# A two-level Winograd matrix product with GELU: one group's B operands are not stored but built again from B, and A is staged in other buffers

## The chip, the cores and the metric

The kernel runs on one core of a Trainium2 chip. The metric is the device time in microseconds (us) of one execution. Five engines work side by side, each through its own instruction stream in order: TensorE (PE, matrix products), VectorE (DVE), ScalarE (ACT), GpSimd (POOL) and SyncE (SP). Here POOL and SP mainly issue DMA transfers. An engine that waits for a semaphore holds up everything behind it in its own stream.

## The reference

```python
def reference(a, b):            # a, b: float32, 4096 x 4096
    x = np.matmul(a, b)
    return 0.5 * x * (1 + np.tanh(np.sqrt(2 / np.pi) * (x + 0.044715 * x**3)))
```

## The kernel before

**The arithmetic.** A, B and the output C are each cut into 2 x 2 quadrants of 2048 x 2048 ("11", "12", "21", "22"). One level of the Winograd form of Strassen's method makes the four quadrants of C from seven products instead of eight. A *group* is one block of C: 512 rows of the upper and 512 of the lower half, 512 columns of the left and 512 of the right half, over the whole depth. There are 4 row blocks (mb) and 4 column blocks (nb), so 16 groups, numbered 0 to 15. Groups 0-3 have mb 0 and nb 0, 1, 2, 3; groups 4-7 have mb 1 and nb 3, 0, 1, 2; groups 8-11 nb 2, 3, 0, 1; groups 12-15 nb 1, 2, 3, 0.

In a group the seven products are called P1 to P7. Each multiplies a 512 x 2048 left operand (a quadrant of A or a sum of some) with a 2048 x 512 right operand (a quadrant of B or a sum of some). P1, P2 and P3 take raw quadrants of B; P4 to P7 take sums. A *full* product has four quarters (q) along the depth, each of four row tiles: 64 matmuls of 128 x 128 by 128 x 512 (line 534). A *split* product applies the same method once more inside: seven quarter products of 16 matmuls with 256 columns (line 908), run in four stages, with four sums of the left operand, four of the right one ("pieces" 5, 6, 7, 4) and some adds and copies in the accumulators between the stages. Operands are float16; a sum of two operands is one DVE instruction over 128 x 2048 (line 838).

**Where B's operands come from.** Groups 1 to 5 are *raw groups* (`raw_group`, line 1293). They load the four quadrants of B for their nb, 64 DMAs of 128 KB on the POOL queue that cast float32 to float16 (`load_raw`, line 1166), and make the sums in place, on top of operands that are no longer needed. The first time that an nb comes up, the seven right operands are also written to DRAM as *units*, 4 x 512 KB each (`keep_`, `store_unit`, on the SP queue). An in-place sum must wait for the store of what it overwrites. Groups 3 and 4 share nb 3. Groups 6 to 15 are *late groups* (`late_group`, line 1407): they fetch units on the POOL queue. How a product is done there is a letter in the table `GROUPS`: no letter is full; "m" is split, with the pieces of the right operand summed in place; "ms" is split, with the pieces also stored to DRAM; "f" is split, with the pieces fetched from DRAM (seven transfers of 512 KB instead of four). `RAW_MAKES` lets group 5 make and store the pieces of P1, P2, P5 and P6 for nb 0.

**Buffers.** A quarter of an operand is a *cell* of 128 x 2048 float16 (512 KB). Cells 0 to 15 hold B (four slots; `bR` in the trace), 16 to 23 sums of A (`SB`, `SA`; `aD`), 24 to 27 the two stages (`ST`; `stage`). In late groups cells 0 to 15 are a pool: `new_cell` takes the first free one, and a fetch waits until the last reader of that cell is done. A transposed quadrant of A lies in four slots (`aT`). While the last group of a row block runs (groups 3, 7 and 11), A for the next row block comes in: `turn_quad` (line 1134) loads half a quadrant (four DMAs of 256 KB) into a stage, DVE transposes it into a slot of `aT` that is no longer used (line 411), and ACT squares it row by row for a check of magnitudes (line 1155). A quadrant's halves alternate between the two stages. In late groups that do not bring in A, the stages hold a sum of A, A11 - A21, the left operand of P7; groups 7 and 11 take four pool cells for that sum instead (`s3 = new_unit()`).

The first raw groups of an nb also sum the squares of B's elements for the same check: 32 ACT squares (line 1189) and 30 DVE adds (line 1194), placed by `SQUARES`.

**The order of the work.** PE's order is as the program writes it. The order on the other engines and on the two DMA queues is set while the kernel is built, by a planner (`Plan`, line 107): each operation has a duration from the table `COST` and each transfer a duration from `MOVE`, with a weight `HEAVY` for the share that a unit's transfer takes of the DMA engines while both queues move data. The planner runs through these durations, lets each engine take the most urgent operation that is ready, and writes down the order. So a different `MOVE` or `HEAVY` moves no work but can change the order on DVE, ACT, POOL and SP everywhere behind group 0.

The outputs leave through `out_of` and `out_from`: an ACT GELU (lines 1099 and 1109) and a 256 KB store on SP. A finished product's accumulators are copied out by ACT (line 1115) or added by DVE to what other products left (line 1121). Where P1 and P2 are full, ACT copies P1's result into P2's accumulators (line 1290), and P2 waits for that copy. In a raw group the products run in the order P1, P2, P5, P6, P7, P4, P3; in groups 7 and 11 P4 comes first.

Of the kernel before, what the change touches and what calls it, by code (L numbers as in the profile page):

```python
# [21 lines left out]
RUN = KC // 4  # L22
RT = 4
# [43 lines left out]
LAG = 0.2  # L67
MARGIN = 1.5
LANES = 8
MOVE = {"unit": 1.27, "out": 0.63, "raw_a": 1.25, "raw_b": 0.65, "tiny": 0.2}  # L70
HEAVY = 1.7
COST = {
    "full": 0.861, "half": 0.876, "wide": 0.983,
    "sum": 1.19, "sum/2": 0.66, "turn": 1.26, "add": 0.68, "add16": 0.69, "small": 0.35, "stat": 2.2,
# [7 lines left out]
def modes_of(tail=None, **kw):  # L82
# [1 line left out]
    return got if tail is None else {**got, "tail": tail}  # L84


RAW_MAKES = {5: ("P1", "P2", "P5", "P6")}
GROUPS = {
    6: modes_of(ms="P2 P5 P7"),
    7: {},  # L90
    8: modes_of(ms="P2 P5 P7"),
    9: modes_of(ms="P2 P5 P7"),
    10: modes_of(f="P1 P2 P5 P6", ms="P7"),
    11: modes_of(m="P5"),
    12: modes_of(f="P2 P5 P7", m="P1 P6"),
    13: modes_of(f="P2 P5 P7", m="P1 P6 P3"),
    14: modes_of(f="P2 P5 P7", m="P1 P6"),
    15: modes_of(f="P1 P2 P5 P6 P7", m="P3"),
}
TURNS = {7: 2, 11: 3}  # L100


# [188 lines left out]
def half_path(  # L291
# [461 lines left out]
    def dma(queue, dst, src, r, w, what, **kw):  # L753
        eng = {"POOL": nc.gpsimd, "SP": nc.sync}[queue]
        weight = HEAVY if what == "unit" else 1.0
        return plan.add(queue, COST[queue], lambda: eng.dma_start(out=dst, in_=src), r=r, w=w, size=MOVE[what],  # L756
                        weight=weight, **kw)

# [372 lines left out]
    rows = [pool.tile([P, 2, NX], F32, name="rows", tag=f"rows{ih}") for ih in range(2)]  # L1131
    seen_rows = set()

    def turn_quad(mb, quad, slot):
        ih, kh = int(quad[0]) - 1, int(quad[1]) - 1
        n = NX // 2
        t = rows[ih]
        for h in range(2):
            k = next_stage[0] % 2
            next_stage[0] += 1  # L1140
            s = stages[k].rearrange("p (x c) r -> p x (c r)", c=CH)
            toks = [c(24 + 2 * k), c(25 + 2 * k)]
            x0 = (ih * MH + mb * TM) // Q + h * n
            batch = (mb, quad, h)
            for g in range(4):
                dma("POOL", s[g * Q : (g + 1) * Q, :, :], a_v[kh, g, :, x0 : x0 + n, :], [], toks,
                    "raw_a", batch=batch)
            for cc in range(CH):
                src = s.rearrange("p x (c r) -> p c x r", c=CH)[:, cc]
                x = slice(h * n, (h + 1) * n)  # L1150
                dve("turn", lambda cc=cc, x=x, src=src: transpose(slot, cc, x, src), toks, [("a", slot, cc, h)])
            f = new_small()
            for x in range(n):
                r = h * n + x
                act("weigh", lambda x=x, r=r, s=s, f=f: nc.scalar.activation(  # L1155
                    small[f].bitcast(F16)[:, : 2 * RUN], s[:, x, :], ACT.Square, accum_out=t[:, kh, r : r + 1]),
                    toks, [("rows", ih), ("f", f)], batch=("w", mb, quad, h), slack=60.0)
            free_small.append(f)
        if (mb, ih) in seen_rows:
            dve("small", lambda: nc.vector.tensor_reduce(  # L1160
                out=stats["a"][:, (2 * mb + ih) * NX : (2 * mb + ih + 1) * NX],
                in_=t.rearrange("p k x -> p x k"), axis=AX.X, op=ALU.add,
            ), [("rows", ih)], [("sa", mb, ih)], slack=60.0)
        seen_rows.add((mb, ih))
# [69 lines left out]
        t = b_phys[x0 // 4, k].rearrange("p j n -> p j n")[:, :, w * HC : (w + 1) * HC]  # L1234
        return t, [c(x0 + 2 * k), c(x0 + 2 * k + 1)]

    spare, behind = [], {}

    def make_raw(nb, name, slot):

        x0 = slot * 4
        prev = {}

        def piece_sum(p, op, x, y):
            t = spare.pop(0)
            combine2(cell(t).rearrange("p (j n) -> p j n", n=HC), [c(t)], x, y, op)
            dma("SP", piece(nb, name, p)[:, :], cell(t), [c(t)], [("t", nb, name, p)], "unit")
            prev[p] = (cell(t).rearrange("p (j n) -> p j n", n=HC), [c(t)])
            spare.append(t)

        b11, b12, b21, b22 = (inner_of(x0, x) for x in ("11", "12", "21", "22"))
        piece_sum("7", -1, b22, b12)
        piece_sum("5", -1, b12, b11)
        piece_sum("6", -1, b22, prev["5"])
        piece_sum("4", -1, b21, prev["6"])
# [36 lines left out]

    def raw_group(gi, keep_units, makes, fetch=(), next_nb=None, turn=None):

        mb, nb = groups[gi]
        X, Y = 0, 1
        sl = dict(slots["b"])
# [15 lines left out]
        block(SB, 1, raw("21"), raw("22"))  # L1313
        block(SA, -1, raw("11"), raw("21"))
        if turn:
            turn_quad(turn, "11", slots["a"]["21"])
        sq("11")
        mk("P1", sl["11"])
        keep_("P1", s11)
# [30 lines left out]

        unsplit(Y, lambda q: a_quarter(blk(SB), q), lambda q: s11[q], True, None, t2)
        if turn:
            turn_quad(turn, "12", slots["a"]["11"])
        mk("P6", sl["11"])
        mk("P4", sl["21"])
        if (gi, "end") in SQUARES:
# [8 lines left out]

        unsplit(X, lambda q: a_quarter(blk(SB), q), lambda q: s11[q], False, u2, s4)
        if turn:
            turn_quad(turn, "21", slots["a"]["12"])
        if next_nb is not None:
            load_raw(next_nb, "11", sl["11"])  # L1370
        elif gi + 1 in REFETCH:
# [9 lines left out]
        unsplit(X, lambda q: a_quarter(blk(SA), q), lambda q: s12[q], False, u3)  # L1381
        if next_nb is not None:
            load_raw(next_nb, "21", sl["12"])
        unsplit(X, lambda q: a_quarter(raw("22"), q), lambda q: s21[q], False, lambda i: out_from(gi, i, 1, 0, X))
        if turn:
            turn_quad(turn, "22", slots["a"]["22"])
        if next_nb is not None:
            load_raw(next_nb, "12", sl["21"])
        elif gi + 1 in REFETCH:
            for q in range(QPH):  # L1390
                fetch_unit_to(nb, "P2", q, s21[q])
# [2 lines left out]
            add_bank(u[i], Y, i)  # L1394
            out_of(gi, i, 0, 1, u[i])

        unsplit(Y, lambda q: a_quarter(blk(SB), q), lambda q: s22[q], False, c12)
        if next_nb is not None:
            load_raw(next_nb, "22", sl["22"])
            slots["b"] = {"11": sl["11"], "21": sl["12"], "12": sl["21"], "22": sl["22"]}  # L1400
# [6 lines left out]
    def late_group(gi, modes, turn=None):  # L1407
# [7 lines left out]
        if new_mb:  # L1415
            block(SA, 1, raw("21"), raw("22"))
        block(SB, -1, blk(SA), raw("11"))
        if turn:
            s3 = new_unit()
            block(s3, -1, raw("11"), raw("21"))  # L1420
            turn_quad(turn, "11", slots["a"]["21"])
        else:
            s3 = ST
            if new_mb:
                block(ST, -1, raw("11"), raw("21"))
        source = {
            "P1": raw("11"), "P2": raw("12"), "P5": blk(SA), "P6": blk(SB), "P7": blk(s3), "P3": blk(SB), "P4": raw("22")
        }
# [50 lines left out]
        if turn:  # L1479
            def p4_done(i, s=X):  # L1480
                x4[i] = copy_out(s, i)

            run(work("P4", X, True, p4_done))
            turn_quad(turn, "22", slots["a"]["22"])
            X, Y = Y, X
        both(("P1", X, True, p1_done, "P6" not in cut), ("P2", Y, not alone, p2_done))
        if last:
            final_answer()
        if turn:
            turn_quad(turn, "12", slots["a"]["11"])  # L1490
        both(("P6", X, False, p6_done, not tail_v), ("P5", Y, True, p5_done, not tail_v))
        if last:
            final_read()
        block(SB, -1, raw("12"), blk(SB))
        if turn:
            turn_quad(turn, "21", slots["a"]["12"])

        def c12(i):
            f = v if tail_v else u
# [47 lines left out]
        if tail_v:  # L1547
            both(("P7", X, True, c22_v, True), ("P3", Y, True, c12))
            if turn:
                free_cells.extend(s3)  # L1550
                for i in range(RT):
                    c21_turn(i)
            else:
                run(work("P4", X, False, c21))
            sets["X"] = Y
        else:
            run(work("P7", X, False, c22))
            if turn:
                free_cells.extend(s3)
                for i in range(RT):  # L1560
                    c21_turn(i)
                run(work("P3", Y, False, c12))
            elif "P3" in cut:
                for i in range(RT):
                    add_bank(u[i], Y, i)
                run(work("P4", X, False, c21), work("P3", Y, True, c12))
            else:
                run(work("P4", X, False, c21))
                run(work("P3", Y, False, c12))
            sets["X"] = X  # L1570
        if turn:
            old = slots["a"]
            slots["a"] = {"11": old["21"], "12": old["11"], "21": old["12"], "22": old["22"]}

    N_RAW = 6
    REFETCH = (4,)
    SQUARES = {(1, q) for q in ("11", "12", "21", "22", "end")} | {(2, q) for q in ("11", "12", "21", "22", "end")}
    SQUARES |= {(3, "12")} | {(4, q) for q in ("11", "21", "22", "end")}
    SQUARES |= {(5, q) for q in ("11", "12", "21", "22", "end")}
    said = {}  # L1580

    def first_weights():
# [42 lines left out]
    with tc.manual_schedule():  # L1625
        nc.vector.memset(zeros[:, :], 0.0)
        first_group()
        behind[1, "P1"] = load_raw(1, "12", slots["b"]["12"])[:8]
        behind[1, "P2"] = load_raw(1, "22", slots["b"]["22"])[8:]
        first_weights()  # L1630
        raw_group(1, NAMES, (), next_nb=2)
        raw_group(2, NAMES, (), next_nb=3)
        raw_group(3, ("P1", "P2", "P5"), (), turn=1)
        spare.extend(ST)
        raw_group(4, ("P3", "P4", "P6", "P7"), (), fetch=("P5", "P7"), next_nb=0)
        raw_group(5, NAMES, RAW_MAKES[5])
        free_small.extend((4, 5, 6, 7))
        for slot in ("11", "12", "21", "22"):
            free_cells.extend(slot_cells(slots["b"][slot]))
        for gi, modes in GROUPS.items():  # L1640
            if gi == LAST:
                final_checks()
            late_group(gi, modes, TURNS.get(gi))
        plan.emit()
# [37 lines left out]
```

## Time and profile before

| | |
|---|---|
| Time, median of 3 runs | 1540.89 us (1539.96 to 1546.77) |
| The profiled execution's own time | 1545.48 us |
| Its span in the trace | 1543.6 us |
| Mean granted TensorE clock | 0.996 of full speed |
| PE idle in the span | 27.7 us |
| Unit fetches (POOL), 512 KB | 274 |
| Piece fetches (POOL), 512 KB | 72 |
| Unit stores and piece stores (SP), 512 KB | 112 and 56 |
| Raw B loads (POOL), 128 KB | 320 |
| Raw A loads of 256 KB (POOL) | 112 |

The profile counts an engine as busy while it executes; DMA issues, waits and branches are not counted. A line of a timeline gives start, duration, engine, source line, operation, tiles and count, and in brackets the idle time before it with the engine that ended it. A line of waits gives the waiting engine and line, the releaser, and then the total us, how often and the longest. A line of a table by stretches gives the stretch and its length, busy us (and instructions) of PE, weight loads, DVE, ACT and POOL, and then PE's granted clock, the DMA share and the GB/s that landed. The DMA share exceeds 1 where packets of two queues overlap.

### The profile page before, as it was taken

To read this page: it belongs to the slowest core of one execution; us is meant where nothing else is said; L and a number is where in the kernel's file an instruction comes from. 1 tells how busy PE (TensorE), PEld (TensorE's weight loads), DVE (VectorE), ACT (ScalarE), POOL (GpSimd) and SP (SyncE) were. 2 spreads that over 40 slices of the span, in tenths; PEclk is the share of its full clock that TensorE was granted. 3 is DMA by queue.
4 is the path that set the end of the run, shared out by engine and by line. 5 is a ranking of instruction groups with operands and counts; after the bars stand their busy time and mean duration, and the time that the engine had idled before them with its cause. 6 is when DMAs were issued, how large, how long until landed. Compare 5 with 4: busy or idle time off the path is not lost.

```text
span 1543.6 us, 24081 instructions
## 1 busy us (share of the span) xinstructions
PE 1515.9 (98%) x9022; PEld 883.6 (57%) x9022; DVE 1024.2 (66%) x1208; ACT 654.8 (42%) x1483; POOL 468.3 (30%) x822
## 2 busy tenths in 40 slices
PE   9999999899999999999899999999999999999998
PEld 4444444344444444664346656686455858877686
DVE  1597865857568399664276657558358877878584
ACT  5447554463864333316553123233573324231333
POOL 7764243442204310123311111233231312223230
PEclk9999999999999999999999999999999999999999
DMA  9999999999949997799987787799996877778794
GB/s 175 194 208 280 334 286 286 310 286 282 214 160 231 301 368 285 263 264 308 250 244 261 283 287 263 254 342 320 298 261 216 292 274 250 260 272 310 258 330 166
DMA packets 201052, 413.79 MB, mean 268 GB/s; under 512 B 20320, under 2 KB 102496, under 8 KB 200928
## 3 DMA queue, kind: packets, MB, share of 16 engines
q0 software_dynamic: 139296, 256.95, 66.7%
q1 hardware_dynamic: 61488, 155.09, 26.7%
q8 instruction: 73, 1.20, 0.3%
q14 instruction: 51, 0.42, 0.1%
q10 hardware_dynamic: 144, 0.13, 0.0%
HBM read 332.40 MB, written 155.19 MB: 316 GB/s over the span
## 4 chain that ended last, share of the span: by engine, by line
PE 75%; DMA 16%; DVE 4%; POOL 2%; issue 2%; ACT 1%; DVEq 0%; SPq 0%; POOLq 0%; ACTq 0%
PE acc L534 45%; PE acc L908 29%; DMA stage<-in_a_dram 7%; DMA bR<-in_b_dram 6%; DMA k_unit<-bR 1%; DVE bR L838 1%; POOL bR L436 1%; DMA bR<-k_unit 1%; DVE y L548 1%; POOL stage L436 1%; DVE aD L838 1%; DVE aD L519 1%; POOL aD L436 0%; DVE stage L838 0%; PE acc L569 0%
## 5 line engine op out<-in xcount | busy, mean ns | idle before, releaser
L534 PE MATMUL acc<-bR,aD 128*128 128x512 f16 x2240 | 495.5, 380 | 9.9 <-DVE bR L838 7.4
L534 PE MATMUL acc<-bR,aT 128*128 128x512 f16 x2048 | 448.6, 380 | 5.4 <-ACT acc L1290 5.4
L534 PEld LDWEIGHTS <-aD 128*128 128x128 f16 x2336 | 228.9, 98 | 284.2 <-issue 18.0
L534 PEld LDWEIGHTS <-aT 128*128 128x128 f16 x2112 | 207.0, 98 | 253.7 <-issue 8.1
L756 POOL DMA_DIRECT2D bR<-k_unit x274 | 166.5, 609 | 558.0 <-PE acc L534 199.5
L908 PE MATMUL acc<-bR 128*128 128x256 f16 x2368 | 276.9, 273 | 1.3 <-DVE bR L838 1.3
L908 PEld LDWEIGHTS <-bR 128*128 128x128 f16 x2368 | 231.6, 98 | 36.6 <-DVE bR L838 1.6
L838 DVE TENSOR_TENSOR bR<-bR 128x2048 f16<-128x2048 f16 x148 | 177.7, 1221 | 90.9 <-DMA bR<-k_unit 28.7
L1121 DVE TENSOR_TENSOR y<-acc,y 128x512 f32<-128x512 f32 x236 | 155.1, 688 | 59.5 <-PE acc L534 33.0
L756 POOL DMA_DIRECT2D bR<-in_b_dram x224 | 121.5, 546 | 199.5 <-DMA bR<-in_b_dram 95.6
L1189 ACT ACTIVATE y<-bR 128x1024 bf16<-128x1024 f16 x128 | 129.4, 1052 | 113.0 <-DVE y L1194 76.1
L411 DVE STREAM_TRANSPOSE aT<-stage 128x1024 uint32<-128x1024 uint32 (+1 forms) x59 | 74.1, 1283 | 134.5 <-DMA stage<-in_a_dram 124.2
L1155 ACT ACTIVATE y<-stage 128x512 f16<-128x512 f16 x192 | 121.2, 631 | 84.9 <-DMA stage<-in_a_dram 74.4
L1099 ACT ACTIVATE y<-y 128x512 f32<-128x512 f32 x188 | 109.5, 625 | 90.3 <-DVE y L1121 88.8
L921 ACT COPY y<-acc 128x256 f32<-128x256 f32 x148 | 55.0, 373 | 200.0 <-PE acc L908 199.8
L925 DVE TENSOR_TENSOR acc<-acc,y 128x256 f32<-128x256 f32 x148 | 62.0, 431 | 80.2 <-PE acc L908 45.2
L1115 ACT COPY y<-acc 128x512 f32<-128x512 f32 x112 | 65.1, 586 | 113.5 <-PE acc L534 82.3
L1194 DVE TENSOR_TENSOR y<-y 128x1024 bf16<-128x1024 bf16 x120 | 82.3, 689 | 33.0 <-ACT y L1189 30.7
L756 POOL DMA_DIRECT2D bR<-k_piece x72 | 39.1, 544 | 177.8 <-PE acc L908 128.1
L908 PE MATMUL acc<-bR,aD 128*128 128x256 f16 x768 | 91.1, 273 | 0.0
L921 ACT COPY acc<-zero 128x256 f32<-128x256 f32 x74 | 27.9, 377 | 135.5 <-DVE y L1121 134.9
L838 DVE TENSOR_TENSOR aD<-aT 128x2048 f16<-128x2048 f16 x52 | 62.1, 1218 | 31.5 <-PE acc L534 31.4
(78 smaller groups left out, 1268.4 us busy)
## 6 DMA issues: line engine op xcount, KB each, us to landing
bR<-k_unit POOLq DMA_DIRECT2D x274, 512.0 KB, 7.5
out_dram<-y SPq DMA_DIRECT2D x251, 256.0 KB, 6.9
k_unit<-bR SPq DMA_DIRECT2D x112, 512.0 KB, 8.8
bR<-in_b_dram POOLq DMA_DIRECT2D x320, 128.0 KB, 7.7
bR<-k_piece POOLq DMA_DIRECT2D x72, 512.0 KB, 6.7
stage<-in_a_dram POOLq DMA_DIRECT2D x112, 256.0 KB, 11.9
k_piece<-bR SPq DMA_DIRECT2D x40, 512.0 KB, 6.5
k_piece<-stage SPq DMA_DIRECT2D x16, 512.0 KB, 9.5
```

The costliest lines, as they stand in the source:

```text
L411: nc.vector.transpose(dst[:, :, x, :], src)
L534: nc.tensor.matmul(acc, sa[:, j // 2, i * P : (i + 1) * P, j % 2], sb[:, j, :], start=start and j == 0, stop=stop and j == 3, skip_group_c ...
L756: return plan.add(queue, COST[queue], lambda: eng.dma_start(out=dst, in_=src), r=r, w=w, size=MOVE[what], weight=weight, **kw)
L838: nc.vector.tensor_tensor(out=dst, in0=xa, in1=ya, op=ALU.add if op > 0 else ALU.subtract)
L908: nc.tensor.matmul(PS[s][i][:, :] if wide else PS[s][i][:, w * HC : (w + 1) * HC], sa[:, j // 2, r * P : (r + 1) * P, j % 2], rhs(j, wide) ...
L921: act(cost, lambda: nc.scalar.copy(out=d, in_=x), [xt] if xt else [], [dt])
L1099: act("gelu", lambda: nc.scalar.activation(t, t, ACT.Gelu_apprx_tanh), [("f", f)], [("f", f)])
L1115: act("copy", lambda: nc.scalar.copy(out=sm(f), in_=bank(s, i)), [], [("f", f), ("p", s, i)])
L1121: dve("add", lambda: nc.vector.tensor_tensor(out=sm(g), in0=bank(s, i), in1=sm(f), op=ALU.add), [("f", f)], [("f", g), ("p", s, i)])
L1155: act("weigh", lambda x=x, r=r, s=s, f=f: nc.scalar.activation(small[f].bitcast(F16)[:, : 2 * RUN], s[:, x, :], ACT.Square, accum_out=t[:, ...
L1189: act("square", lambda t=t, src=src: nc.scalar.activation(t, src, ACT.Square), [c(cx)], [("f", f)], slack=60.0)
L1194: dve("add16", lambda t=t, u=u: nc.vector.tensor_tensor(out=u, in0=u, in1=t, op=ALU.add), [("f", f)], [("f", e)], slack=60.0)
```

## The change

Group 1 stores none of its right operands. Nb 1 comes up again at group 6, five groups on, which becomes a raw group: group 5 loads its B from the input at its end, and group 6 makes the operands and stores the 28 units. Group 1's squares for the check move to group 6.

In the raw groups 1, 2, 4, 5 and 6 P3 is split, with its pieces summed in place. P4's four quarters alternate with P3's four stages. The temporary cells are the stages, which these groups do not need otherwise.

Fewer pieces go through DRAM: `RAW_MAKES` is empty, group 10 splits P2, P5 and P7 only (and stores their pieces), group 12 sums all its pieces itself, and group 15 splits five products instead of six. Counted over the program, there are 36 split products instead of 37, 384 raw B loads instead of 320, 291 fetches of 512 KB instead of 346, and 36 piece stores instead of 56; unit stores stay at 112.

In all late groups the sum A11 - A21 stays in `ST`, and A is staged in pool cells instead: four cells, as two stages, taken from the pool for the length of the group. In group 7 the order of the quadrants becomes 22, 11, 12, 21 (it was 11, 22, 12, 21); for the last row block quadrant 11 is brought in during group 10 already (`EARLY`), and 22, 12 and 21 in group 11. The planner's numbers for transfers change too.

```diff
-MOVE = {"unit": 1.27, "out": 0.63, "raw_a": 1.25, "raw_b": 0.65, "tiny": 0.2}
-HEAVY = 1.7
+MOVE = {"store": 1.33, "fetch": 1.42, "out": 0.66, "raw_a": 1.35, "raw_b": 0.68, "tiny": 0.2}
+HEAVY = 1.8
...
-RAW_MAKES = {5: ("P1", "P2", "P5", "P6")}
+RAW_MAKES = {}
+RAW_CUT = (1, 2, 4, 5, 6)
 GROUPS = {
-    6: modes_of(ms="P2 P5 P7"),
     7: {},
...
-    10: modes_of(f="P1 P2 P5 P6", ms="P7"),
+    10: modes_of(ms="P2 P5 P7"),
     11: modes_of(m="P5"),
-    12: modes_of(f="P2 P5 P7", m="P1 P6"),
+    12: modes_of(m="P2 P5 P7 P1 P6"),
...
-    15: modes_of(f="P1 P2 P5 P6 P7", m="P3"),
+    15: modes_of(f="P2 P5 P7", m="P1 P6"),
 }
+EARLY = {10: 3}
...
-            k = next_stage[0] % 2
+            k = pairs[next_stage[0] % len(pairs)]
             next_stage[0] += 1
-            s = stages[k].rearrange("p (x c) r -> p x (c r)", c=CH)
-            toks = [c(24 + 2 * k), c(25 + 2 * k)]
+            s = chunk(k).rearrange("p (x r) -> p x r", r=CH * RUN)
+            toks = [c(k), c(k + 1)]
...
-        unsplit(X, lambda q: a_quarter(raw("22"), q), lambda q: s21[q], False, lambda i: out_from(gi, i, 1, 0, X))
+        p4 = (X, lambda q: a_quarter(raw("22"), q), lambda q: s21[q], False, lambda i: out_from(gi, i, 1, 0, X))
+        if not cut:
+            unsplit(*p4)
...
-        unsplit(Y, lambda q: a_quarter(blk(SB), q), lambda q: s22[q], False, c12)
+        if cut:
+            for i in range(RT):
+                add_bank(u[i], Y, i)
+            b = made_here(s22, new_cell, lambda p: None, free_cells.append)
+            run(quarters(*p4), stages_of(split(Y, blk(SB), b, True), c12))
+            if next_nb is not None:
+                load_raw(next_nb, "12", sl["21"])
+        else:
+            unsplit(Y, lambda q: a_quarter(blk(SB), q), lambda q: s22[q], False, c12)
...
-        if turn:
-            s3 = new_unit()
-            block(s3, -1, raw("11"), raw("21"))
-            turn_quad(turn, "11", slots["a"]["21"])
-        else:
-            s3 = ST
-            if new_mb:
-                block(ST, -1, raw("11"), raw("21"))
+        s3 = ST
+        if new_mb:
+            block(ST, -1, raw("11"), raw("21"))
+        if gi in EARLY or turn:
+            k = new_unit()
+            pairs = (k[0], k[2])
+        if gi in EARLY:
+            turn_quad(EARLY[gi], "11", slots["a"]["21"], pairs)
+            free_cells.extend(k)
...
-    N_RAW = 6
+    N_RAW = 7
...
-        raw_group(1, NAMES, (), next_nb=2)
+        raw_group(1, (), (), next_nb=2)
...
-        raw_group(5, NAMES, RAW_MAKES[5])
+        raw_group(5, NAMES, RAW_MAKES.get(5, ()), next_nb=1)
+        raw_group(6, NAMES, RAW_MAKES.get(6, ()))
```

## The prediction

> **What bounds the kernel now.** I read the busy times first, then who made TensorE wait, then TensorE's own timeline for where, then stretches of time by engine for why.
>
> ```profile
> span 1543.6 us, 24081 instructions
> ...
> PE 1515.9 (98%) x9022; PEld 883.6 (57%) x9022; DVE 1024.2 (66%) x1208; ACT 654.8 (42%) x1483; POOL 468.3 (30%) x822
> ```
>
> TensorE (PE) is the bound: every other engine is idle a third of the time or more. So a change is worth the PE work it adds or removes, plus the PE idle time it adds or removes. The waits of PE and the places in its timeline (idle time in brackets):
>
> ```profile
> PE acc L534 <- DVE bR L838: 7.4, 2, 5.2
> PE acc L534 <- ACT acc L1290: 5.4, 2, 4.2
> PE acc L534 <- ACT y L1109: 2.2, 3, 1.0
> ```
> ```profile
> 176.88 17.54 PE L534 MATMUL acc<-bR,aD 128*128 128x512 f16 x80 [2.27 <-DVE bR L838]
> ...
> 250.95 1.89 PE L534 MATMUL acc<-bR,aD 128*128 128x512 f16 x8 [0.41 <-ACT y L1109]
> 253.81 18.29 PE L534 MATMUL acc<-bR,aD 128*128 128x512 f16 x84 [0.98 <-ACT y L1109]
> 277.28 12.93 PE L534 MATMUL acc<-bR,aD 128*128 128x512 f16 x49 [5.18 <-DVE bR L838]
> ```
> ```profile
> 743.01 15.42 PE L534 MATMUL acc<-bR,aT 128*128 128x512 f16 x64 [4.16 <-ACT acc L1290]
> ```
>
> By group (a full product is 64 matmuls, 221.88-208.07 = 13.8 us, a full group 7 x 13.8 = 96.7): group 1 loses 2.27, group 2 0.41+0.98+5.18 = 6.57, group 5 0.85, group 7 4.16, group 8 0.20, group 11 1.19, group 13 1.30. The long stalls cost a second time, because the granted clock drops behind them:
>
> ```profile
> 160.00:180.00 20.00, 17.73 (x83) 7.94 (x82) 13.86 (x15) 8.91 (x28) 3.60 (x7) 1.00 1.10 337
> 260.00:280.00 20.00, 14.82 (x64) 6.39 (x62) 17.40 (x18) 3.17 (x3) 4.82 (x9) 0.87 1.08 348
> 280.00:300.00 20.00, 20.00 (x90) 8.86 (x89) 16.45 (x20) 11.94 (x15) 7.65 (x15) 0.96 1.13 295
> 740.00:760.00 20.00, 16.99 (x73) 7.38 (x73) 4.17 (x4) 13.76 (x38) 5.79 (x11) 0.91 1.17 231
> ```
>
> The third last number is the clock. From 260 to 300 PE did 154 matmuls; 34.8 us not idle hold 161 at 0.216, so 1.6 us were lost. Group 7 lost 0.8 likewise (255 for 259 from 720 to 780). Behind the 2.27 us stall the clock stayed 1.00. Stalls behind group 0 thus cost 16.5 + 2.4 = **19 us**, of which group 2 is 8.2 and group 7 5.0.
>
> Why group 2? Its DMA engines are full. The last two columns here are DMA share and GB/s:
>
> ```profile
> 122.00:222.00 100.00, 97.73 (x452) 44.08 (x451) 76.22 (x90) 66.18 (x132) 36.13 (x67) 1.00 1.13 301
> 222.00:328.00 106.00, 99.44 (x450) 44.38 (x448) 65.20 (x75) 52.28 (x87) 42.08 (x79) 0.97 1.13 298
> 425.00:516.00 91.00, 91.00 (x423) 41.26 (x422) 61.40 (x70) 45.14 (x68) 23.81 (x44) 1.00 0.77 213
> ```
>
> Both groups run at 1.13 throughout. At 221.9, where group 2 starts, 32 of its 64 raw B loads are still to be issued; the last goes out at 259, and the in-place sums that need it run at 273.7, so the fourth product waits. At group 5 (start 521.2) 22 loads are late, the last at 546, and only 0.85 is lost. That pair is my gauge.
>
> **The change, part by part.**
>
> *Prices of DMA (estimates).* 560 to 580 moved 417 GB/s, nearly all stores and fetches of 512 KB: 1.26 us each. 40 to 60 moved 195 GB/s, all raw loads: 128 KB of raw B is 0.67, 256 KB of raw A 1.34. An output is 0.63. Held against the trace: 222 to 273 issued 14 stores, 33 raw B, 1 raw A, 8 outputs: 46 of 51 us.
>
> *Group 1 stores nothing.* Before, group 1 asks for 28 stores (35.3), 64 raw B (42.9) and 16 outputs (10.1) = 88 us, on top of up to 32 raw loads (21) carried in from group 0: 110 in 97 us. Now it is 53 + 21 = 74. The 2.27 us wait for a store ahead of an in-place sum goes (-2.27), and group 2 starts without a backlog. Its own demand stays 88 in 95.4 us.
>
> *P3 split in raw groups 1, 2, 4, 5 (and 6).* Seven quarter products of 16 matmuls of 256 columns replace 64 of 512: 112 x 0.1096 (480 took 52.61) = 12.28, plus two wide matmuls at +0.106 each. Over all groups: four gain a split product; group 6 goes from 3 to 1, 10 from 5 to 3, 15 from 6 to 5. That is one split product fewer, 48 matmuls fewer, and 8 more wide parts: (13.81-12.28) + 8 x 0.106 = **+2.4 us** of PE work. Nothing hides it.
>
> *What the split does to the next loads.* P4's quarters now alternate with P3's stages, so the buffers of P4's second half come free some 3 us before the group's end, not 14; the first half of P3's comes 6 us before it, the second at its end, as before. In the new order of the POOL queue the loads behind these points are 24 (8 of quadrant 12, 16 of 22): 16 us of DMA, done some 25 us into the next group with the stores of P1 and P2 (8 x 1.26 = 10) beside them. The sums need them 34 to 47 us in. By the gauge (22 late: 0.85; 32 late: 8.2) I keep 1.0 each at groups 2 and 6, 0.9 at 5, 0.5 at 3. Bounds: 0 and 8.2 each.
>
> *VectorE in raw groups.* +8 sums at 1.16 (4.62 for 4), +4 adds at 0.61, +4 part adds at 0.38: 13 us. Group 2 has 65 of 106 busy, so 78 of 95; group 1 loses its 30 squares' adds; group 5 loses 16 sums and had run 80.9 of 98 with one small stall. Hidden; without cover, 13 us a group.
>
> *Group 6 is raw.* 28 fetches and 12 piece stores (50 us) go, 28 stores come (35), and 64 raw loads come into group 5 (43), which drops 16 pieces (20). Group 5 asks 88 in 95.4, as group 2 does. Its squares (32 on ACT at 1.05, 30 adds on DVE) move in from group 1; ACT was 42% busy.
>
> *A staged in pool cells.* In group 7 the "22" halves are first, in cells that come free in group 6, and land before the group. The stall there is this:
>
> ```profile
> 739.48 0.63 ACT L1155 ACTIVATE y<-stage 128x512 f16<-128x512 f16 x1 [5.38 <-DMA stage<-in_a_dram]
> ...
> 742.38 2.04 ACT L1290 COPY acc<-acc 128x512 f32<-128x512 f32 x4
> ```
>
> ACT executes in order; the copies that seed P2's banks stand behind squares of a half that landed late. In the new order one square of the third half still stands ahead of three copies. That half can be loaded only once P4 and two transposes are done, 15 us into the group; with 11.9 us from issue to landing it comes at 27 to 29, and the copy is due at 27.6. So 0 to 5: I take 2.0 (it was 5.0). Group 11 loads one quadrant in group 10 now: 1.19 becomes 0.3.
>
> *Groups 10, 12, 15.* Fetches fall by 12, 9 and 6: DMA was at 0.78, worth nothing on PE. Group 12 makes three products' sums itself: 12 x 1.16 = 13.9 us on DVE, 70.6 of 89 becomes 84.5. Group 11 in front drops four sums and four transposes (9.3 us) and had 57.6 of 97, so blocks for group 12 can be made early. I take 0.5 (0 to 6); group 13 keeps 1.3.
>
> *Sum against the profiled execution (span 1543.6, its time 1545.5).* Stalls of 19.0 become 1.0+0.5+0.9+1.0+2.0+0.3+0.5+1.3 = 7.5 (groups 2, 3, 5, 6, 7, 11, 12, 13). Net -19.0 + 7.5 + 2.4 = -9.1: 1536.4. The profiled execution is 4.6 over the median of the runs (1540.9), so I take the same step from the median: **1532**.
>
> **The rivals.**
>
> *A. Late loads at every raw boundary (slower).* The split frees buffers late, and group 3 also has A halves queued between its B loads. If groups 3, 5 and 6 each stall like group 2 did (8.2), that adds 3 x 8.2 - (0.5+0.9+1.0) = 22: 1554. It decides once some 30 loads are outstanding at a group's start. For: group 2 of before. Against: there the queue carried a backlog of over 20 us, now none. Two such boundaries pay back the gain, three make it slower by 0.8%. 0.20.
>
> *B. Half the gain.* Group 7 keeps its 5.0 and groups 2 and 6 lose 3 us each: +7, 1539. For: both sit on DMA landings that the new order still puts first. 0.20.
>
> *C. DVE bounds group 12.* If the early blocks do not fit, 84.5 us with their waits cost about 6: 1538. For: group 13, at 68 of 88, already shows a 1.30 wait on DVE. 0.08.
>
> *D. Not relieved.* If the stalls return elsewhere in full, only the added PE work remains: 1543. 0.04.
>
> *E. A memory limit.* Raw loads read float32, so from 222 to 273 HBM carried 33 x 0.262 + 14 x 0.524 + 8 x 0.262 + 0.524 = 18.6 MB, 364 GB/s, more than the 293 that landed. If that is a ceiling, groups 2 and 5 need (64 x 0.262 + 28 x 0.524 + 16 x 0.262 = 35.7 MB) 98 us for 95.4: +2.6 each, 1537. Against it stand the 417 GB/s of 560 to 580. 0.03.
> The Trainium skill (DMA: Bandwidth & Descriptors, Specifications) gives some 358 GB/s of HBM for each core; by it the 35.7 MB take an estimated 100 us, 4 over each such group, and the sum would be some 1540. The trace speaks against it with 417 GB/s over 20 us.
>
> **How the numbers follow.** Forecast (1525 to 1533): 0.45. B, C, D and E end within 0.5% (7.7 us, about what a measurement of this kernel can tell): 0.35. A: 0.20. If all stalls behind group 0 vanished, -19.0 + 2.4 gives 1524, the floor. The low end is 1525; the high end 1549 takes in B to E and the milder half of A. Faster 0.45, same 0.35, slower 0.20.
>
> **What would show it.** PE's matmuls fall by 48 to 8974. No PE wait near 177 us; group 2 idles 1 to 2 us instead of 6.57, and the clock there stays 1.00. DMA share from 122 to 222 is clearly under 1.13. The copy at the start of group 7 waits 0 to 3. I am wrong if PE shows a wait of over 3 us for a DVE sum some 40 us into groups 3, 5 or 6, or repeated waits for DVE in group 12.

## The result, and the profile after

The changed kernel takes **1529.56 us** (median of 4 runs, 1527.87 to 1530.25). The kernel before, run beside it, takes 1542.64 (1539.96 to 1546.77). The ratio is 0.9911 with a 95% interval of 0.9885 to 0.9937: faster by 0.6 to 1.2%. The profiled execution after took 1530.25, with a granted clock of 0.999 (0.996 before).

The page of after, first lines and busy times:

```profile
span 1528.7 us, 23988 instructions
...
PE 1515.7 (99%) x8974; PEld 878.8 (57%) x8974; DVE 1053.6 (69%) x1236; ACT 653.9 (43%) x1483; POOL 460.9 (30%) x831
```

PE has the 48 matmuls less that were forecast and is busy for as long as before; the span is shorter because PE idles 13.0 us instead of 27.7. DVE works 29 us more, and nothing waits for that. Who makes PE wait in after, behind group 0:

```profile
PE acc L535 <- DMA bR<-k_unit: 2.4, 1, 2.4
...
PE acc L535 <- ACT y L1112: 0.8, 2, 0.4
```

The waits for an in-place sum (`DVE bR`, 7.4 us before) and for the seeding copy (`ACT acc`, 5.4) are gone. On PE's timeline of after, only three lines behind group 0 have idle time in front:

```profile
341.35 1.02 PE L535 MATMUL acc<-bR,aD 128*128 128x512 f16 x4 [0.41 <-ACT y L1112]
342.78 39.87 PE L535 MATMUL acc<-bR,aD 128*128 128x512 f16 x184 [0.41 <-ACT y L1112]
...
998.87 5.30 PE L535 MATMUL acc<-bR,aT 128*128 128x512 f16 x16 [2.39 <-DMA bR<-k_unit]
```

The stalls behind group 0 fell from 16.5 us to 0.41 + 0.41 + 2.39 = 3.2. The last line holds a loss that no bracket shows: 16 matmuls took 5.30 us, where 16 like them take 3.62 elsewhere, so the clock cost 1.7 more.

The stretches of after by group (groups 1, 2, 5 and 12) and three 20 us windows; the last three columns are clock, DMA share and GB/s:

```profile
122.00:217.00 95.00, 95.00 (x496) 48.40 (x495) 67.71 (x71) 39.28 (x109) 40.65 (x76) 1.00 0.89 185
217.00:312.00 95.00, 95.00 (x496) 48.30 (x494) 73.78 (x85) 42.06 (x60) 33.92 (x63) 1.00 1.06 285
...
505.00:601.00 96.00, 96.00 (x504) 49.05 (x502) 78.00 (x92) 49.06 (x69) 34.34 (x64) 1.00 1.08 286
...
740.00:760.00 20.00, 20.00 (x95) 9.05 (x93) 9.36 (x9) 13.35 (x36) 7.28 (x13) 1.00 1.16 280
160.00:180.00 20.00, 20.00 (x94) 9.02 (x93) 15.99 (x16) 2.68 (x5) 7.27 (x14) 1.00 0.46 64
1000.00:1020.00 20.00, 20.00 (x128) 12.76 (x127) 13.25 (x13) 6.74 (x14) 3.16 (x6) 0.92 0.81 282
1169.00:1258.00 89.00, 88.97 (x689) 67.17 (x688) 80.16 (x96) 25.41 (x61) 15.48 (x28) 1.00 0.62 213
```

Group 1 moves 185 GB/s instead of 301, and from 160 to 180, where the first sum was late before, DMA is at 0.46 instead of 1.10. Group 2 starts with half the backlog: 16 raw loads late instead of 32, the last one issued at 235.7 instead of 259. PE is busy for all of groups 1, 2 and 5, and group 12 survives 80 us of DVE work in 89.

Between the last matmuls' ends (1538.3 before, 1523.6 after) lie -14.7 us: stalls -13.3, clock -2.0 (3.6 before, 1.7 after), group 0 -0.9, PE work +2.4 (by the starts of the matmuls), and a rest of -0.9. Nearly all of the rest comes from how a bracket is counted: it begins where the last matmul's 0.38 us end, some 0.16 us after the next one would have started (full matmuls start 0.216 us apart), and there were nine such stalls before and three after.

### The profile page after: what moved, and what is told of

Read it like the earlier page. It is cut to its first block, busy times and chain, and to the rows that moved or that the text cites. A ratio compares the mean times of both kernels' runs of the same rounds, so it can differ in the third digit from the quotient of the medians.

```text
span 1528.7 us, 23988 instructions
## 1 busy us (share of the span) xinstructions
PE 1515.7 (99%) x8974; PEld 878.8 (57%) x8974; DVE 1053.6 (69%) x1236; ACT 653.9 (43%) x1483; POOL 460.9 (30%) x831
## 4 chain that ended last, share of the span: by engine, by line
PE 89%; DMA 6%; DVE 2%; POOL 1%; issue 1%; ACT 1%; ACTq 0%; POOLq 0%; DVEq 0%
PE acc L535 59%; PE acc L911 27%; PE acc L570 2%; DMA stage<-in_a_dram 2%; DMA bR<-in_a_dram 2%; DMA bR<-in_b_dram 2%; DMA bR<-k_unit 1%; POOL stage L437 1%; DVE y L549 1%; DVE aD L520 1%; POOL bR L437 0%; DVE aT L412 0%; ACT y L1158 0%; DVE aD L549 0%; POOL bR L759 0%
## 5 line engine op out<-in xcount | busy, mean ns | idle before, releaser
L535 PEld LDWEIGHTS <-aD 128*128 128x128 f16 x2272 | 222.4, 98 | 264.6 <-issue 4.9
L841 DVE TENSOR_TENSOR bR<-bR 128x2048 f16<-128x2048 f16 x181 | 218.0, 1221 | 84.7 <-DMA bR<-in_b_dram 38.1
L911 PE MATMUL acc<-bR 128*128 128x256 f16 x1984 | 232.4, 273 | 0.0
L759 POOL DMA_DIRECT2D bR<-in_b_dram x288 | 155.4, 544 | 250.2 <-PE acc L535 154.0
L911 PEld LDWEIGHTS <-bR 128*128 128x128 f16 x1984 | 194.1, 98 | 30.6 <-DVE bR L841 0.3
L911 PE MATMUL acc<-bR,aD 128*128 128x256 f16 (+1 forms) x864 | 103.8, 274 | 0.0
L1158 ACT ACTIVATE y<-bR 128x512 f16<-128x512 f16 x128 | 80.5, 629 | 38.1 <-DMA bR<-in_a_dram 29.2
L841 DVE TENSOR_TENSOR aD<-aT,aD 128x2048 f16<-128x2048 f16 x60 | 72.9, 1220 | 32.3 <-PE acc L535 32.3
L841 DVE TENSOR_TENSOR aD<-aD,aT 128x2048 f16<-128x2048 f16 x60 | 72.5, 1220 | 29.0 <-PE acc L535 29.0
L911 PEld LDWEIGHTS <-aD 128*128 128x128 f16 x864 | 84.5, 98 | 13.0
L412 DVE STREAM_TRANSPOSE aT<-stage 128x1024 uint32<-128x1024 uint32 (+1 forms) x27 | 35.7, 1349 | 63.3 <-DMA stage<-in_a_dram 53.8
```

Source lines behind the costliest of these rows:

```text
L535: nc.tensor.matmul(acc, sa[:, j // 2, i * P : (i + 1) * P, j % 2], sb[:, j, :], start=start and j == 0, stop=stop and j == 3, skip_group_c ...
L841: nc.vector.tensor_tensor(out=dst, in0=xa, in1=ya, op=ALU.add if op > 0 else ALU.subtract)
L911: nc.tensor.matmul(PS[s][i][:, :] if wide else PS[s][i][:, w * HC : (w + 1) * HC], sa[:, j // 2, r * P : (r + 1) * P, j % 2], rhs(j, wide) ...
```

## The experiments

Each is timed against the kernel before on its own chip. Before scatters widely (medians 1548.40, 1549.82 and 1550.74 on the three later chips, single runs from 1539 to 1561), after hardly: its repeat below took 1530.01 on a second chip. So I also set each time against after's 1529.6 to 1530.0, and read the reasons from the traces. After itself was not run on the chip of the first four experiments, nor on that of the last four: there a difference from after is one across chips. Three theories stood against each other: the relief of group 1's stores makes the gain; the staging of A in pool cells makes it; or the planner's new numbers, which reorder every engine, make it.

**The planner's numbers alone.** The kernel before with the two new lines of numbers (and the lines that tell a store from a fetch):

```diff
-MOVE = {"unit": 1.27, "out": 0.63, "raw_a": 1.25, "raw_b": 0.65, "tiny": 0.2}
-HEAVY = 1.7
+MOVE = {"store": 1.33, "fetch": 1.42, "out": 0.66, "raw_a": 1.35, "raw_b": 0.68, "tiny": 0.2}
+HEAVY = 1.8
...
```

> The kernel before with the new transfer numbers (MOVE, HEAVY) alone: the same work in another order. If the relief of the DMA engines made the gain (theory T: traffic), groups 1 and 2 stay overfull: 1538 to 1546 us, with some 6 to 9 us of PE idle time still between 120 and 290 us. If the better numbers made it (theory N: numbers), the late landings are foreseen: 1529 to 1534, and the waits behind ACT in groups 7 and 11 are gone.

Measured: 1543.12 (1532.94 to 1545.68), ratio 0.9955 [0.9926, 0.9984]. PE's timeline of this run, its stalls of over 0.8 us in groups 1, 2 and at the end of 7:

```profile
172.85 3.61 PE L534 MATMUL acc<-bR,aD 128*128 128x512 f16 x16 [1.87 <-DVE bR L840]
177.30 17.43 PE L534 MATMUL acc<-bR,aD 128*128 128x512 f16 x80 [0.84 <-DVE bR L840]
...
275.90 22.17 PE L534 MATMUL acc<-bR,aD 128*128 128x512 f16 x96 [4.29 <-DVE bR L840]
...
796.34 16.16 PE L534 MATMUL acc<-bR,aD 128*128 128x512 f16 x64 [5.14 <-DVE y L1123]
```

The numbers alone gain something, but not the change's gain. The ten runs spread widely; the profile is of one at 1543.35. The copies of P1's result in groups 7 and 11 no longer make PE wait; a new stall of 5.14 stands at the end of group 7. The stalls of groups 1 and 2, the ones by traffic, stay. DVE's timeline of the same run shows what stood ahead of the 5.14:

```profile
784.17 2.37 DVE L411 STREAM_TRANSPOSE aT<-stage 128x1024 uint32<-128x1024 uint32 x2 [5.47 <-DMA stage<-in_a_dram]
786.47 4.59 DVE L840 TENSOR_TENSOR aD<-aT 128x2048 f16<-128x2048 f16 x4
790.97 4.62 DVE L840 TENSOR_TENSOR stage<-aT 128x2048 f16<-128x2048 f16 x4
795.51 0.18 DVE L1162 TENSOR_REDUCE stat_a<-rows 128x16 f32<-128x32 f32 x1
795.61 1.87 DVE L1123 TENSOR_TENSOR y<-acc,y 128x512 f32<-128x512 f32 x3
```

The add that PE needs (L1123) stands behind transposes that waited 5.47 us for A to land, and behind eight sums. It is the stall of group 7 of before on another engine. This picture comes back in six of the runs below.

**The structure alone.** After with the old numbers (the diff above, reversed).

> The changed kernel with the old transfer numbers. Theory T: 1528 to 1534, at most 4 us over the changed kernel. Theory N: 1537 or more, with waits behind ACT in groups 7 and 11 as before.

Measured: 1537.77 (1536.21 to 1540.04), ratio 0.9936 [0.9911, 0.9961], 8 us over after. The two largest stalls, and what ACT did ahead of the first:

```profile
330.92 15.65 PE L535 MATMUL acc<-bR,aT 128*128 128x512 f16 x64 [3.03 <-ACT acc L1291]
...
789.74 14.04 PE L535 MATMUL acc<-bR,aD 128*128 128x512 f16 x64 [2.54 <-DVE y L1122]
```
```profile
325.14 0.63 ACT L1156 ACTIVATE y<-stage 128x512 f16<-128x512 f16 x1 [4.72 <-DMA stage<-in_a_dram]
...
330.30 1.55 ACT L1291 COPY acc<-acc 128x512 f32<-128x512 f32 x3
```

Groups 1 and 2 have no stall, so the structure alone cures those. What the new numbers add lies mostly where A comes in, in groups 3 and 7. In group 3 ACT waited 4.72 us for a stage to land, squared it for 5 us, and only then made the copies that P2 needs. The time is the one expected if the numbers made the gain, as the time of the run before was the one expected if the traffic made it: neither theory is the whole.

**Group 1 stores again.** After, but:

```diff
-        raw_group(1, (), (), next_nb=2)
+        raw_group(1, NAMES, (), next_nb=2)
```

> The changed kernel, but group 1 also stores its 28 units, which group 6 then stores again (14.7 MB more). Theory T: DMA share 1.13 again from 122 to 222 us, 28 or more late raw loads at the start of group 2, 8 to 11 us of stalls in groups 1 and 2: 1537 to 1541. If the traffic of group 1 was not the cause: within 3 us of the changed kernel.

Measured: 1542.37 (1540.22 to 1545.66), ratio 0.9973 [0.9950, 0.9995]: 12.8 over after, but still 6.0 under before on this chip. PE's timeline:

```profile
165.46 7.07 PE L535 MATMUL acc<-bR,aD 128*128 128x512 f16 x32 [2.44 <-DVE bR L841]
174.54 22.57 PE L535 MATMUL acc<-bR,aD 128*128 128x512 f16 x96 [2.02 <-DVE bR L841]
370.56 23.68 PE L535 MATMUL acc<-bR,aD 128*128 128x512 f16 x96 [3.53 <-DVE bR L841]
```

The sums are late again, in group 1 and, new, in group 3. The DMA share is 1.12 from 122 to 222, 1.10 from 222 to 320 and 1.11 from 320 to 420: the queue stays full through two more groups, until the one where A halves join it. In group 3 the DVE sums themselves waited 1.90 us for `in_b_dram`. The relief of group 1 carries most of the gain: stalls behind group 0 and the clock behind them cost 16.0 us in this profile, 20.1 in before's and 4.9 in after's.

**The staging undone.** After, but A is staged in `ST` and the sum A11 - A21 takes pool cells in groups 7 and 11 as before; no early quadrant, quadrant 11 first:

```diff
-EARLY = {10: 3}
+EARLY = {}
...
-        if gi in EARLY or turn:
-            k = new_unit()
-            pairs = (k[0], k[2])
...
+        pairs = (24, 26)
+        if turn:
+            s3 = new_unit()
+            block(s3, -1, raw("11"), raw("21"))
+            turn_quad(turn, "11", slots["a"]["21"], pairs)
...
```

> The changed kernel with the staging of A undone: stages in ST, the sum for P7 in pool cells, quadrant 11 first, no early quadrant in group 10. Theory T (staging is a small part): group 7 gets back 3 to 5 us behind ACT and group 11 about 1, group 10 loses its 4 us of wait and clock: 1529 to 1534. If staging was the main part (theory S): 1537 or more.

Measured: 1541.75 (1536.69 to 1549.91), ratio 0.9955 [0.9924, 0.9986], 12.2 over after and 6.7 under before on this chip. PE's stalls at the end of group 7 and in group 11, then ACT's timeline ahead of the second:

```profile
784.65 15.53 PE L535 MATMUL acc<-bR,aD 128*128 128x512 f16 x64 [3.54 <-DVE y L1124]
...
1110.23 16.57 PE L535 MATMUL acc<-bR,aT 128*128 128x512 f16 x64 [5.99 <-ACT acc L1293]
```
```profile
1107.46 0.63 ACT L1158 ACTIVATE y<-stage 128x512 f16<-128x512 f16 x1 [5.83 <-DMA stage<-in_a_dram]
...
1109.60 1.55 ACT L1293 COPY acc<-acc 128x512 f32<-128x512 f32 x3
```

A square that waits 5.83 us for A stands ahead of the seeding copies: group 7 of before, now in group 11. These two stalls and the clock behind them, (3.54 + 1.6) + (5.99 + 2.6) = 13.7, exceed the difference. So the staging is not the small part that one theory had, but is worth about as much as the relief. The two do not add up: each, undone alone, costs most of the gain of the change.

**After again, P3 full, and no early quadrant.** Three kernels on one chip: after unchanged, after with `RAW_CUT = ()`, after with `EARLY = {}`.

> The changed kernel itself, as the control on the chip that runs the next three. Both theories: ratio to the kernel before between 0.988 and 0.994, PE waits behind group 0 of 2 to 5 us in sum.

> The changed kernel with P3 full in groups 1, 2, 4, 5 and 6. PE has 5 x 1.53 - 10 x 0.106 = 6.6 us more to do. Theory T with hidden late loads: no PE wait over 1 us is added or removed at the starts of groups 2, 3, 5 and 6, so 5 to 8 us over the control. Rival A (the split frees buffers late and that costs): the waits at group 3 go and the loss is under 4 us.

> The changed kernel with all of A for the last row block brought in during group 11, still in pool cells. If the wait of group 10 (2.39 us and the clock behind it, some 4 us) comes from the cells and fetch slots that the early quadrant takes there, it goes; group 11 gets 1 to 3 us behind ACT: within 3 us of the control. If the early quadrant is what cleared group 11: 4 us or more over the control, with ACT's copy at the start of group 11 waiting.

Measured: after 1530.01 (1527.17 to 1532.99), ratio 0.9893 [0.9852, 0.9934]; P3 full 1535.73 (1532.32 to 1542.69), 0.9914 [0.9883, 0.9944]; no early quadrant 1535.42 (1534.00 to 1539.49), 0.9914 [0.9883, 0.9946].

With P3 full the time rises by 5.7, as the added PE work (6.6) says, and PE waits for no sum of a raw group with or without the split: its late loads do no harm, and rival A's mechanism is not there. With P3 full the raw groups have no stall at all; after again has 2.2 us in group 3, all behind ACT, and by these two profiles that is the most that the split costs beside its work. Without the early quadrant group 10 has no stall, and group 11 gets a larger one, at its end and behind DVE, not at its start behind ACT as was expected. PE's timeline of that run (its profiled execution took 1539.49, 4.1 over its median), and DVE's ahead of it:

```profile
1160.47 15.66 PE L535 MATMUL acc<-bR,aD 128*128 128x512 f16 x64 [5.02 <-DVE y L1124]
```
```profile
1153.91 2.37 DVE L412 STREAM_TRANSPOSE aT<-bR 128x1024 uint32<-128x1024 uint32 x2 [4.87 <-DMA bR<-in_a_dram]
1156.20 3.46 DVE L841 TENSOR_TENSOR aD<-aT 128x2048 f16<-128x2048 f16 x3
1159.73 2.48 DVE L1124 TENSOR_TENSOR y<-acc,y 128x512 f32<-128x512 f32 x4
```

Here too transposes waited for A ahead of the add that PE needed. The early quadrant costs group 10 between 0.4 and 4 us (0.38 of wait in the repeat, 2.39 + 1.7 in after's first profile) and saves group 11 over 6 in that execution.

**Group 9 splits P1 and P6.** A try for a faster version:

```diff
-    9: modes_of(ms="P2 P5 P7"),
+    9: modes_of(ms="P2 P5 P7", m="P1 P6"),
```

> The changed kernel with P1 and P6 split in group 9 too, pieces summed in place: 2 x 1.53 = 3.1 us less PE work there, 20 more DVE sums and adds (some 23 us of DVE in a group that has it 55 to 60 busy of 92). If DVE has room: 2 to 4 us under the control. If cells or DVE run short: PE waits for DVE or for fetches in group 9 eat it, 0 to 4 us over the control.

Measured: 1528.94 (1528.78 to 1531.18), ratio 0.9888 [0.9850, 0.9926]; against after on the same chip -1.1, not told apart from none. PE's work fell by 3.1, but group 10 now waits twice for fetches: 0.50, and 2.25 with the clock behind it.

```profile
996.66 5.30 PE L535 MATMUL acc<-bR,aT 128*128 128x512 f16 x16 [2.25 <-DMA bR<-k_unit]
```

**Two cells instead of four for the early quadrant, and more splits.** The first of these kernels has this edit; the others add `m="P1 P6"` in group 9, in 8 and 9, and in 8, 9 and 10.

```diff
-            turn_quad(EARLY[gi], "11", slots["a"]["21"], pairs)
-            free_cells.extend(k)
+            free_cells[:0] = k[2:]
+            turn_quad(EARLY[gi], "11", slots["a"]["21"], pairs[:1])
+            free_cells.extend(k[:2])
```

> After, but the early quadrant of group 10 is staged through two cells instead of four. In after, group 10's first matmuls waited 2.39 us on a fetch of a stored B block and then 16 of them took 5.30 us instead of 3.62, which is 4 us at most (0.4 us in the repeat of after, and nothing with no early quadrant). Theory: the fetch is late because the staging holds the cell that it lands in, so with two cells fewer taken the wait of group 10 is gone: 0.4 to 4 us faster than after (some 1526 to 1529 where after takes 1530). Rival: the two halves of the quadrant now follow each other through the same cells, the second later, and group 11 starts later by the wait that no early quadrant gives (up to 5 us): 1530 to 1535. Rival: the fetch is late by its place in the queue, not for the cell: the wait stays at 0.4 to 2.4 and the time is that of after.

> The run before this one, and group 9 forms P1 and P6 as sums of products where after multiplies their own operands, as groups 0 to 7 mostly do: 3.1 us of PE's work less, and DVE of that group at 73 of 89 us instead of 52, as the run with group 9 split on its own showed (1528.94, with 2.75 us of wait for a fetch at group 10). Theory: what that run gave back was the wait at group 10 by cells; with two cells it gains the whole 3.1 us, some 1523 to 1527. Rival: DVE's added work holds the cells longer, the fetch is late with either staging, and the time stays at 1528 to 1530.

> As the run before, with group 8 split too: 6.1 us of PE's work less than after in all, DVE at 73 to 78 of some 91 us in groups 8 and 9. Theory that PE bounds and DVE is only crowded where it is over nine tenths of a group: another 3 us faster than with group 9 alone, some 1520 to 1525. Rival: the fetches of groups 9 and 10, which stand behind more stores and sums, come late and bring waits of 2 to 6 us: 1524 to 1531.

> As the run before, with group 10 split too: 9.2 us of PE's work less than after, the early quadrant of group 11 staged in the same group, so that DVE of group 10 comes to some 80 us or more of 92. Theory that PE bounds: 1517 to 1523. Rival: DVE's sums stand ahead of the transposed copies of the early quadrant, group 10 ends or group 11 starts with a wait of 3 to 6 us and the gain of the third split is lost: 1521 to 1530.

Measured, in this order: 1531.41 (1529.15 to 1538.82), ratio 0.9871 [0.9839, 0.9904]; 1541.06 (1539.38 to 1542.50), 0.9936 [0.9910, 0.9962]; 1537.40 (1532.94 to 1543.66), 0.9925 [0.9892, 0.9958]; 1535.32 (1533.37 to 1537.96), 0.9905 [0.9878, 0.9932]. The last three took longer than every expectation, the rivals' too. The theory fell in the first: group 10 waits for its fetch as in after. This is PE's timeline with two cells:

```profile
999.60 5.30 PE L535 MATMUL acc<-bR,aT 128*128 128x512 f16 x16 [3.03 <-DMA bR<-k_unit]
```

The number of cells that the staging takes is not what makes the fetch late. The fetches ahead of it left at 981.2 to 988.2, most of them when PE had read what lay in the cell, and in after at 981.1 to 988.1. With the old planner numbers the quadrant comes in as early and PE does not wait there at all, so the order of the queue has a part in it. What orders the fetches is not settled further.

With two cells and group 9 split, the stall is worse by far. PE's timeline, and DVE's:

```profile
1000.69 3.59 PE L911 MATMUL acc<-bR 128*128 128x256 f16 x16 [6.58 <-DVE bR L841]
1008.12 6.04 PE L535 MATMUL acc<-bR,aT 128*128 128x512 f16 x16 [3.84 <-DMA bR<-k_unit]
```
```profile
996.40 2.37 DVE L412 STREAM_TRANSPOSE aT<-bR 128x1024 uint32<-128x1024 uint32 x2 [4.15 <-DMA bR<-in_a_dram]
999.40 1.22 DVE L841 TENSOR_TENSOR bR<-aT 128x2048 f16<-128x2048 f16 x1 [0.63 <-ACT y L1158]
```

The second half of the quadrant has to follow the first through one stage; it left at 979.6 to 984.0, and DVE stood before its transposes until 996.4, with the sum that PE needed behind them. With groups 8 and 9 split the same place loses 4.91 and 5.02, and the end of group 7, ahead of the split groups, 3.95. With all three it loses 12.73, again behind transposes, which waited 6.21 us for A. Up to 9.2 us of PE's work were taken out, and none of these three beats after. DVE was not full there: 73 us of 96 in group 10 of the last (88 of 92 in its group 8, where PE had no wait). No version tried beats after by more than the measurement can tell.

## Why the prediction was right, and where its steps were off

The forecast of 1532 was 2.4 above the result. Part of that closeness is luck. From profiled execution to profiled execution I forecast -9.1 and got -15.2. The step of 4.6 from the profiled execution to the median made up for it: after's profiled execution lies 0.7 over its median, and before's, with the one run added, 2.8.

- **PE bounds, and idle time decides**: right. The change in PE's matmul work was the +2.4 of the forecast, and all the gain is idle time and clock. The split P3 spares 6.6 us of PE work, and with full products the time rose by 5.7.
- **Group 1's relief**: right, and worth about as much as the staging of A. The wait near 177 us is gone and group 2 starts with half the late loads. That the backlog would reach as far as group 3 when group 1 stores was not seen.
- **Residual stalls, 7.5**: mis-sized; 3.2 were measured, and not in the places named. Groups 2, 5, 6, 11, 12 and 13 have 0 instead of 1.0, 0.9, 1.0, 0.3, 0.5 and 1.3. Group 2 had 16 loads late instead of 24, because the last left 19 us into the group and not 25. In group 3, 21 B loads were late and 0.82 was lost (0.5 forecast), by the wait for ACT's GELU and not for a sum. That the gauge (22 late: 0.85) gives the same is no support for it: its own 0.85, at group 5 of before, was a wait for ACT's GELU too, and with P3 full 19 loads were late in group 3 and nothing was lost. Before's line:

```profile
549.85 41.60 PE L534 MATMUL acc<-bR,aD 128*128 128x512 f16 x192 [0.85 <-ACT y L1109]
```

- **Group 7, 2.0**: it lost nothing. The third half landed 24 us into the group, not 27 to 29, and the square that stands ahead of the copies was done just in time. ACT's timeline of after shows it: the copy waits only for PE.

```profile
720.33 0.63 ACT L1158 ACTIVATE y<-bR 128x512 f16<-128x512 f16 x1 [6.48 <-DMA bR<-in_a_dram]
...
721.37 0.57 ACT L1293 COPY acc<-acc 128x512 f32<-128x512 f32 x1 [0.31 <-PE acc L535]
```

- **The early quadrant, -0.9 in group 11**: the step that failed most. It is worth 5.4 us, and with it comes the one large new stall, at group 10, which I had at nothing because DMA there was at 0.78. In after it was at 0.92 from 960 to 1060, and one fetch was late all the same: a mean share over a group does not say when one fetch behind others in a queue lands.
- **The clock, 2.4**: too small. I counted matmuls in windows (64 + 90 from 260 to 300), and a window also counts those that lie across its edges: by the trace 151 start there, so 10 are short and not 7. Timed as groups, the 96 matmuls behind the stall in group 2 took 23.07 instead of some 20.9 (64 take 13.98 and 128 take 27.79), and the 64 in group 7 15.42 instead of 13.98: 3.6.
- **The planner's numbers**: I gave them no term of their own. With the old ones the same structure takes some 8 us more.
- **The rivals.** A fell: its late loads do cost time when there is a backlog (group 3 with group 1's stores, 3.53 and the clock behind it), but the split does not make them. B and C fell: groups 2, 6 and 7 lose nothing, and DVE at 80 of 89 us in group 12 bounds nothing. D was right in kind for each kernel with one part undone, where stalls moved on to other groups, and wrong for the whole. E fell: groups 2 and 5 carry the 35.7 MB in 95 us without a stall, 375 GB/s. The Trainium skill (HBM Reference, Specifications (TRN2)) says that a core streaming alone measures well above its share of 358 GB/s, some 425; that agrees with the 417 of the prediction (nearly all stores) and with these groups.

## What to carry to other kernels

Where the engine that bounds a kernel is busy 98% of the time, look for waits on a DMA in the streams of the *other* engines, and for what stands behind them: in the stalls followed back here in groups 3, 7, 10 and 11, ACT or DVE waited 4 to 6 us for a raw load with the copy, add or sum that PE needed next in line behind it. Loading such data a group earlier is worth more than the load's own wait suggests, and a planner's durations, which move no work, can be worth some 8 us because they decide what stands behind what. Parts of a change that relieve one queue do not add up: undo one, and most of the gain can go.

## What the runs showed of the hardware

Behind a stall the clock can halve, and the stall's length does not say alone whether it does. By their starts in the trace, the full matmuls then come 0.427 us apart for a time (eight of the 16 in group 10 of after) and after that 0.216 again. Behind waits of 2.02, 2.25 and 2.39 us this cost 1.7 us each time; behind 1.87, 2.27, 2.44 and 2.54 nothing; behind each wait of 3 us or more between 1.3 and 2.9. The wait of 1.85 us at the end of group 0, which all 14 profiles have, cost 1.7 in two of them (the staging undone, and groups 8, 9 and 10 split) and nothing in twelve. So a stall of 2 us may cost 2 or 3.7, in the same kernel: with group 1's stores, the wait of 2.44 cost nothing more and the shorter one of 2.02 behind it 1.7.

The Trainium skill (TensorE: Matmul & The Clock Gate, Part 1) tells of a free-running window of 3.41 us and of half the clock after at least one idle window. One window at half the clock would cost an estimated 1.7 us, which is what the short waits cost where they cost anything, and a window that runs freely may be why equal waits cost unequally; but here waits well under a window were enough, and on that the measurement decides.

Before's single runs on one chip spread over 20.5 us (31 runs, 1539.79 to 1560.30), after's over 5.8 on another (4 runs, 1527.17 to 1532.99). That before scatters because it waits so often for landings is likely and was not shown.
